# RWKV scores, chain and outputs of a two-layer hybrid mixer as products per head

## The chip, the cores and the metric

The kernel runs on one core of a Trainium2 chip. The metric is the device time of one execution in microseconds (us), as the median of several runs. The core has TensorE (PE; its weight loads are listed as PEld), VectorE (DVE), ScalarE (ACT), GpSimd (POOL) and the queue of SyncE (SP), from which most transfers are started. They run side by side and wait for each other by semaphores.

## What is computed

The reference is a network of two layers over 256 text and 1024 image tokens with 1024 channels. Each layer projects its normed input to four mixers (RWKV-7, S5, SSD and GLA), runs each in both directions over the tokens, and projects their outputs back. The change touches the RWKV mixer alone. It has 4 heads of 64 channels; for each direction and head a state S of 64 x 64 goes through the tokens, and the outputs of both directions are added:

```python
def step(S, inp):
    r_t, w_t, k_t, v_t, kk_t, a_t = inp
    sa = jnp.einsum('bhvk,bhk->bhv', S, -kk_t)
    S = S * w_t[:, :, None, :] + sa[..., None] * (kk_t * a_t)[:, :, None, :] + v_t[..., None] * k_t[:, :, None, :]
    y = jnp.einsum('bhvk,bhk->bhv', S, r_t) if need_out else None
    return S, y
...
y = ys[0] + ys[1]
```

A norm over each head, a bonus term and a gate follow. The kernel does the recurrence in chunks of 64 tokens: within a chunk as products with masked scores and the inverse of a triangular matrix, from chunk to chunk with S.

## The kernel before

A layer has three phases: the projections with the mixers other than RWKV and S5 (`project`), RWKV with S5 beside it (`rw`), and the projection out (`out_proj`). `rw` goes through 10 windows. A window is 128 tokens (two chunks, s = 0 and 1) of the forward direction and 128 of the backward one, whose tokens are reversed, so that both run as one. u = 0 to 3 counts direction (u // 2) and pair of heads (u % 2); a pair of heads h = 0, 1 fills the 128 partitions. Each window goes through five stages, and iteration i traces stage st of window i - st, in the order 3, 2, 4, 1, 0 (`ORDER`):

- stage 0, `rw_elem` (L1169): decays, keys and receptances by channel. It loads the window, makes two sets of decay products in the PSUM tag `ps`, whose results ScalarE's tanh reads (L1188), and writes `r_AR` (per chunk 64 columns of keys times decay and 64 of receptance times decay), `r_BK` and the decays `r_PM` of whole chunks;
- stage 1, `rw_pair` (L1232): the scores A of a chunk. GpSimd spreads AR into the zeroed tile `r_AD`, each head in its own columns and partitions (L1242); a product of 128 rows and 256 columns per chunk and pair of heads goes to the tag `pb` (L1246); VectorE masks it into `r_A` (L1248). Then the keys by token, `r_Bt`;
- stage 2, `rw_inv` (L1271), the inverses `r_TT`, with products of 32 x 32 in the tag `pi` and much VectorE work on `r_N`, `r_X` and `r_tp`, and `rw_vals` (L1330): the values into the lower half of `r_UV`, whose upper half GpSimd clears (L1346);
- stage 3, `rw_chain` (L1349): the recurrence over the two chunks. In `px`: a product with zeros that opens the bank (L1359), A times UV (L1362), AR times the state S (L1367). Two copies to `r_rs`, by VectorE and ScalarE (L1371, L1372). In `pu`: TT times rs (L1375), copied into the upper half of UV (L1376, L1377), and Bt times UV (L1382), added to the decayed state (L1389, L1390). Then the chunk's outputs by token, A times UV in the other half of px's rows (L1394), copied to `r_yw` (L1397);
- stage 4, `rw_out` (L1401): a product with the constant `IJ` (identity and reversed identity) turns yw to channels in a bank of `ps` and undoes the reversal of the backward direction (L1410); its result is copied or added into `r_yt` (L1419, L1421). `rw_final` (L1423) does norm, bonus and gate, when both directions have come to a block; it takes banks of `ps` too.

`PS` gives the PSUM banks by tag: px 2, pu 1, p5 1, pi 1, pb 2, ps 1. A new tile of a tag waits until a bank of it is free. All products are f32 and stand in the trace as two records each. Almost all are issued by the helper `mm` (L321), and elementwise work by `tt` (L333), `ts` (L336), `stt` (L339) and `act` (L330), so that lines say little and tiles are the better name. The order on each engine is not that of the text: the framework's planner (`schedule_with_timeline_sim`, L1810) lays it by priorities in the order of the text and its own estimate of times.

Of the kernel before, what the change touches and what calls it, by code (L numbers as in the profile page):

```python
# [11 lines left out]
F32 = mybir.dt.float32  # L12
# [20 lines left out]
# ---------------------------------------------------------------- column layout of w_in  # L33
# [30 lines left out]
# ---------------------------------------------------------------- per-layer parameter columns  # L64
# [24 lines left out]
for _d, _l in ((CON, [("ident", 128), ("ones", 128), ("bones", 128), ("eps", 1), ("gneps", 1), ("one", 1)]),  # L89
               (ACON, [("triF", 128), ("triB", 128), ("gmF", 64), ("gmB", 64), ("bm4", 4), ("c16", 16), ("reset64", 256)]),  # L90
               (RCON, [("IJ", 128), ("vinit", 256), ("rm", 128), ("m16", 32), ("reset64", 256)])):
    _o = 0
    for _n, _c in _l:
        _d[_n] = (_o, _c)
        _o += _c
# [6 lines left out]
def constants():  # L102
# [24 lines left out]
    ij = np.zeros((128, 128))  # L127
    ij[64:, :64] = np.eye(64)
    ij[:64, 64:] = np.eye(64)[::-1]
    put("IJ", ij)  # L130
# [93 lines left out]
# PSUM banks by tag: projections of the first layer and of the others, RWKV, out-projection  # L224
# [16 lines left out]
AA = "ppvv"  # L241
# engines of RWKV's elementwise work, by step: a ACT, p GpSimd, v DVE
EG = dict(bk="aa", ad="pppp", dg="aaaa", bb="pp", b0="p", b1="v", tk="pp", am="p", ar="vp", sp="p", bt="aa")
# [12 lines left out]
class K:  # L256
# [17 lines left out]
    def load_con(self, rwkv):  # L274
        """the constants and matrices of a phase"""
# [8 lines left out]
    def pools(self, es, nts=0, nq=0, nh=0, left=(), right=(), **psum):  # L284
        """the pools of a phase: by name, from either end of SBUF; PSUM banks by tag"""
# [23 lines left out]
    def ring(self, name, shape, n):  # L309
        """n tiles in turn, zeroed once: what is written later leaves the zeros alone"""  # L310
# [12 lines left out]
    # short names of engine operations  # L323
# [29 lines left out]
    def rsqrt(self, tag, in_, scale, eps):  # L353
        """1 / sqrt(in * scale + eps) of a few numbers per partition: a guess from the bits, Newton's steps"""
# [10 lines left out]
    def head_norm(self, tag, ps, sq, scale, eps):  # L365
        """ps: 1 / sqrt(mean of sq over its head + eps), by channel; its first columns hold the sums by token"""
# [8 lines left out]
    def y_out(self, Y, jobs, row, scale):  # L375
        """token-major Y (list of [128, 5, 256]) -> rows row.. of the stash, channels times scale[i]"""
# [12 lines left out]
    # ------------------------------------------------------------ GLA  # L389
    def gla(self, src, outs):  # L390
# [22 lines left out]
        for d in range(2):  # L413
# [16 lines left out]
            # chain factor of step s: exp(cs_mid of the next chunk + cs_last - cs_mid of this one)  # L430
# [21 lines left out]
        for s in range(20):  # L452
            ch = [s, 3 - s if s < 4 else 23 - s]
            jb = [x // 2 for x in ch]
            if s % 2 == 0:
                # keys by token, one half of the rows zero
# [11 lines left out]
            if s > 0 and (outs or s >= 4):  # L468
                # one direction is in the first half of its block of 128 tokens, the other in the second
# [15 lines left out]
            # state within each head; decayed, and spread over the columns of all heads  # L485
# [11 lines left out]
        # norm over each head, gate  # L497
# [16 lines left out]
    def gla_pair(self, j, qe, ke, pa, V, Y):  # L514
        """interactions within the two chunks of 128 tokens, both directions"""
# [22 lines left out]
    # ------------------------------------------------------------ SSD  # L538
    def ssd(self, src, outs):
        nc, c = self.nc, self.c  # L540
        jobs = list(range(0 if outs else 2, 10))
        # centred convolution in the padded axis, silu
# [12 lines left out]
        # strict triangles  # L555
# [4 lines left out]
        # dt and decays by token  # L560
# [16 lines left out]
        # the same in two parts  # L577
# [25 lines left out]
        # decays of the state by step, heads of a half of the partitions  # L603
# [7 lines left out]
        for s in range(10):  # L611
# [26 lines left out]
            # state within each head; spread over the columns of all heads  # L638
# [26 lines left out]
    def ssd_pair(self, j, B, C, cp, xt, stri, lap, dt, Y):  # L665
        """interactions within a chunk, both directions"""
# [6 lines left out]
        # decays of both directions: each leaves the other's triangle alone  # L673
# [37 lines left out]
    def s5_prep(self, l):  # L711
        """matrices of 8 tokens and phases of chunks for the scan, by quarters of 4 groups, out to DRAM"""
# [190 lines left out]
    def s5_jobs(self, outs):  # L903
# [7 lines left out]
        y = []  # L911
# [902 lines left out]
```

## Time and profile before

| | us |
|---|---|
| median of 3 runs | 2290.6 |
| lowest, highest | 2287.16, 2292.19 |
| span of the profiled execution | 2282.5 |
| PE busy in it | 1955.0 (86%) |
| DVE busy | 1565.4 (69%) |
| ACT busy | 933.8 (41%) |
| POOL busy | 830.7 (36%) |

The profile shows one execution from its first to its last instruction; the runs' time has also what lies around it. PE's time is the union of its records, whose ends are modelled. RWKV's phases are seen from the first load of decays to the last output: from 708 to 1142 us in the first layer and from 1768 to 2172 us in the second.

### The profile page before, as it was taken

The numbers are of one execution on the slowest core, as the hardware profiler recorded it, in microseconds if no ns is written. First come the engines' busy times: TensorE is split into PE (matmuls) and PEld (weight loads), VectorE is DVE, ScalarE is ACT, GpSimd is POOL, SyncE is SP. The second block draws the span as 40 slices with busy tenths as digits, with TensorE's granted clock in tenths as the row PEclk, the third lists the DMA queues.
The fourth block names the chain that finished last, engine by engine and source line by source line (L and its number), as shares of the span: only waits on it lengthen the run. The fifth ranks groups of instructions, "written<-read, shape, count | busy, mean of one in ns | idle before, by whom it ended". The sixth has DMA issues, their size and how long they took to land.

```text
span 2282.5 us, 44172 instructions
## 1 busy us (share of the span) xinstructions
PE 1955.0 (86%) x17176; PEld 1642.1 (72%) x17176; DVE 1565.4 (69%) x3513; ACT 933.8 (41%) x2016; POOL 830.7 (36%) x947
## 2 busy tenths in 40 slices
PE   7788898999975587878899999999996567888997
PEld 5577787778743466766799888887884456767797
DVE  3986867547495888897647724366665799987654
ACT  3445222223442554645423326122463456565420
POOL 1434753302246444553332203220136355454322
PEclk8689999999997688979999999999997678899898
DMA  8133544224454322422233423132412432220432
GB/s 281 44 116 122 179 152 136 65 91 140 149 164 136 112 83 80 121 64 68 94 116 94 137 90 133 55 99 86 146 50 73 145 97 85 80 75 25 139 112 93
DMA packets 208481, 246.79 MB, mean 108 GB/s; under 512 B 28816, under 2 KB 150672, under 8 KB 208272
## 3 DMA queue, kind: packets, MB, share of 16 engines
q1 hardware_dynamic: 175264, 215.52, 29.8%
q10 hardware_dynamic: 33008, 28.45, 3.8%
q8 instruction: 135, 2.21, 0.4%
q14 instruction: 74, 0.61, 0.1%
HBM read 169.29 MB, written 76.71 MB: 108 GB/s over the span
## 4 chain that ended last, share of the span: by engine, by line
PE 36%; DVE 17%; ACT 6%; issue 3%; DMA 3%; POOL 2%; SPq 0%; ACTq 0%; DVEq 0%; POOLq 0%
PE pj L321 22%; PE ps L321 3%; PE px L321 2%; PE pu L321 2%; DVE r_tp L333 2%; DVE r_X L333 2%; PE pb L321 2%; PE pc L321 1%; PE pi L321 1%; DVE r_N L1276 1%; DVE r_cs L1195 1%; PE p L321 1%; DVE z_x L333 1%; DVE r_BK L333 1%; ACT r_th L330 1%
## 5 line engine op out<-in xcount | busy, mean ns | idle before, releaser
L321 PE MATMUL pj<-hi,i_wh 128*128 128x512 f32 (+1 forms) x952 | 243.8, 377 | 18.6 <-DVE hi L1516 12.0
L321 PE MATMUL pj<-lo,i_wh 128*128 128x512 f32 (+1 forms) x952 | 240.2, 370 | 1.3 <-POOL lo L333 1.3
L321 PE MATMUL pj<-hi,i_wl 128*128 128x512 f32 (+1 forms) x952 | 239.1, 369 | 0.1
L321 PEld LDWEIGHTS pj<-hi,i_wh 128*128 128x128 f32 x952 | 169.1, 196 | 52.3 <-DVE hi L1516 12.4
L321 PEld LDWEIGHTS pj<-lo,i_wh 128*128 128x128 f32 x952 | 167.3, 193 | 32.5 <-issue 1.5
L321 PEld LDWEIGHTS pj<-hi,i_wl 128*128 128x128 f32 x952 | 167.0, 192 | 31.2 <-issue 2.6
L333 DVE TENSOR_TENSOR i_wl<-i_w,i_wh 128x512 fp32r<-128x512 f32 x108 | 82.6, 772 | 107.8 <-PE pj L321 59.9
L1539 ACT CAST i_wh<-i_w 128x512 fp32r<-128x512 f32 x108 | 66.4, 620 | 159.0 <-PE pj L321 113.4
L321 PE MATMUL pb<-r_AD,r_BK 128*128 128x256 f32 x320 | 99.9, 464 | 19.9 <-DVE r_tp L333 9.4
L321 PE MATMUL px<-r_UV,r_A 128*64 128x64 f32 x1216 | 103.9, 240 | 14.1 <-DVE r_UV L1376 10.5
L321 PEld LDWEIGHTS px<-r_UV,r_A 128*64 128x64 f32 x1216 | 88.1, 150 | 35.0 <-DVE r_UV L1376 14.6
L321 PEld LDWEIGHTS pb<-r_AD,r_BK 128*128 128x128 f32 x320 | 72.0, 237 | 37.6 <-issue 11.9
L333 DVE TENSOR_TENSOR r_X<-r_X,r_tp 128x30 f32<-128x30 f32 (+1 forms) x300 | 89.8, 299 | 6.7
L333 DVE TENSOR_TENSOR r_tp<-r_N,r_X 128x30 f32<-128x30 f32 (+1 forms) x300 | 87.6, 292 | 6.6
L321 PE MATMUL pu<-r_rs,r_TT 128*64 128x128 f32 x320 | 51.2, 311 | 35.0 <-ACT r_rs L1372 35.0
L330 ACT ACT_TABLE_LOAD x56 | 71.8, 1283 | 11.6 <-DMA z<-in_s5p 4.6
L330 ACT ACTIVATE i_o<-pj,omu 128x512 f32<-128x512 f32 (+1 forms) x46 | 28.5, 622 | 115.4 <-PE pj L321 113.8
L333 DVE TENSOR_TENSOR g_Y<-pc,g_Y 64x256 f32<-64x256 f32 x70 | 29.5, 421 | 65.0 <-ACT g_Y L536 35.3
L333 POOL TENSOR_TENSOR r_S<-r_S,r_PM 64x256 f32<-64x256 f32 x72 | 53.0, 737 | 56.6 <-DVE r_S L333 43.1
L321 PE MATMUL pj<-i_wh,hi 128*128 128x256 f32 x448 | 67.2, 288 | 6.4 <-ACT i_o L330 4.0
L336 POOL TENSOR_SCALAR r_AD<-r_AR 64x512 f32<-64x512 f32 (+1 forms) x80 | 56.7, 709 | 40.8 <-PE pb L321 31.9
L321 PEld LDWEIGHTS pu<-r_rs,r_TT 128*64 128x64 f32 x320 | 40.1, 155 | 41.4 <-ACT r_rs L1372 39.5
(458 smaller groups left out, 5172.6 us busy)
## 6 DMA issues: line engine op xcount, KB each, us to landing
i_w<-in_win SPq DMA_DIRECT2D x108, 256.0 KB, 3.0
i_o<-in_ada SPq DMA_DIRECT2D x96, 256.0 KB, 4.6
r_in<-rm SPq DMA_DIRECT2D x36, 512.0 KB, 4.2
rm<-i_o SPq DMA_DIRECT2D x48, 256.0 KB, 2.5
o_y<-yd SPq DMA_DIRECT2D x36, 256.0 KB, 3.2
z_st<-s5t SPq DMA_DIRECT2D x32, 256.0 KB, 2.7
o_w<-in_wout SPq DMA_DIRECT2D x32, 256.0 KB, 2.9
z_st<-s5t SPq DMA_DIRECT2D x24, 320.0 KB, 5.1
```

The costliest lines, as they stand in the source:

```text
L321: self.nc.tensor.matmul(out, lhsT, rhs, start=start, stop=stop, skip_group_check=True)
L330: self.nc.scalar.activation(out=out, in_=in_, func=f, **kw)
L333: (self.nc.vector if e == "v" else self.nc.gpsimd).tensor_tensor(out, a, b, op)
L336: (self.nc.vector if e == "v" else self.nc.gpsimd).tensor_scalar(out, a, s1, s2, op0, op1)
L1195: nc.vector.tensor_tensor_scan(cs[:, v], c("reset64"), t2[:, v], 0.0, OP.mult, OP.add)
L1276: nc.vector.transpose(Nt[:, :1024].rearrange("p (i j) -> p i j", j=32), AD.rearrange("p u t -> p t u").unsqueeze(2).to_broadcast([128, 32, ...
L1539: self.nc.scalar.copy(hi[:, v], w)
```

## The change

Comments and docstrings are left out of the new file; they are not shown. In `rw_pair`, r_AD and its copies go: each head's score product takes its own 64 partitions of BK and AR, 128 columns wide (64 in windows that give no outputs), and each head has its own bank. In `rw_chain` each product is taken per head with 64 output rows, which go to the lower or upper half of the bank's partitions by head; the opening product goes, rs is one tile of 128 partitions copied by VectorE alone, and the outputs leave the step. `rw_out` is called at the end of `rw_chain`: it makes the outputs by channel directly, S times the receptances and UV times A, and reverses the backward tokens when it writes them. IJ and yw go, UV has two buffers, S three.

```diff
@@ rw_pair
-        for d in range(2):
-            z = self.rzero("r_AD", [128, 2, 2, 2, 2, 64], 1)
+        hs = [slice(64 * h, 64 * h + 64) for h in range(2)]
+        for s in range(2):
+
+            ps = [self.P("pb").rearrange("p (u f) -> p u f", u=4) for _ in hs]
+            for u in range(4):
+                for h in range(2):
+                    self.mm(ps[h][:, u, :n], BK[hs[h], u, s].rearrange("p k t -> p (k t)"),
+                            AR[hs[h], u // 2, u % 2, s, :n // 64].rearrange("p k t -> p (k t)"))
             for h in range(2):
...
+                self.tt(A[:, s, :, h, :n], ps[h][:, :, :n], c("rm")[:, :n].unsqueeze(1).to_broadcast([128, 4, n]), OP.mult)
@@ rw_vals
-        UV = self.rzero("r_UV", [128, 2, 4, 128], 1)
+        UV = self.R("r_UV", [128, 2, 4, 128], 2)
@@ rw_chain
...
+            X = self.P("px")[:, :256].rearrange("p (u v) -> p u v", u=4)
+            for u, h in uh:
+                self.mm(X[hs[h], u], A[:, s, u, h, 0:64], UV[:, s, u, hs[h]], u == 0, S is None and u == 3)
             if S is not None:
...
+                for u, h in uh:
+                    self.mm(X[hs[h], u], AR[:, u // 2, u % 2, s, 0], S[:, u, hs[h]], False, u == 3)
+            rs = self.R("r_rs", [128, 4, 64], 2)
+            nc.vector.tensor_copy(rs, X)
+            ps = self.P("pu")[:, :256].rearrange("p (u v) -> p u v", u=4)
+            for u, h in uh:
+                self.mm(ps[hs[h], u], TT[hs[h], s * 4 + u], rs[hs[h], u])
+            nc.vector.tensor_copy(UV[0:64, s, :, hs[0]], ps[hs[0]])
+            nc.scalar.copy(UV[0:64, s, :, hs[1]], ps[hs[1]])
             Sn = None
...
+                X2 = self.P("pu")[:, :256].rearrange("p (u v) -> p u v", u=4)
+                for u, h in uh:
+                    self.mm(X2[hs[h], u], Bt[:, s, u, hs[h]], UV[:, s, u, hs[h]])
+
+                Sn = self.rzero("r_S", [128, 4, 128], 3)
...
             S = Sn
+        if need:
+            self.rw_out(W, at)
         return S
@@ rw_out
+        for s, S in enumerate(at):
+            for u in range(4):
+                o = ps[:, s, u % 2, u // 2]
+                if S is not None:
+                    for h in hs:
+                        self.mm(o[h], S[:, u, h], AR[:, u // 2, u % 2, s, 1], True, False)
+                for i, h in enumerate(hs):
+                    self.mm(o[h], UV[:, s, u, h], A[:, s, u, i, 64:128], S is None, True)
...
             if d:
-                o = o[:, :, ::-1]
+                o = o[:, :, ::-1, ::-1]
```

## Rows read from the trace of the kernel before

**Rows 1.** Busy us (instructions) of PE, PEld, DVE, ACT, POOL by stage, granted clock, DMA.
```profile
708.00:1142.00 434.00, 329.16 (x3891) 272.08 (x3892) 349.06 (x764) 224.15 (x532) 205.37 (x262) 0.83 0.29 90
1768.00:2172.00 404.00, 318.04 (x3812) 266.44 (x3811) 337.00 (x753) 219.13 (x522) 183.94 (x241) 0.84 0.30 92
```

**Rows 2.** Chain of waits from 708 to 1142 us, share of that stretch by line.
```profile
by line: issue 6.9%; PE px L321 6.1%; DVE r_tp L333 6.0%; DVE r_X L333 5.7%; PE pu L321 5.1%; PE pb L321 5.1%; PE ps L321 4.7%; PE pi L321 3.5%; PE p L321 3.5%; DVE r_N L1276 3.1%; DVE r_cs L1195 2.9%; ACT r_TT L1315 2.3%; DVE z_b L333 2.1%
```

**Rows 3.** Chain of waits from 1768 to 2172 us, share of that stretch by line.
```profile
by line: issue 8.6%; PE pu L321 6.8%; PE px L321 6.2%; DVE r_tp L333 5.5%; DVE r_X L333 5.3%; DVE z_x L333 3.4%; PE pb L321 3.3%; DVE r_BK L333 3.1%; DVE r_N L1276 2.9%; PE ps L321 2.6%; PE pi L321 2.5%; ACT r_th L330 2.5%; DVE r_cs L1195 2
```

**Rows 4.** Busy us by stage, as in the first group, for shorter stretches.
```profile
760.00:800.00 40.00, 26.46 (x276) 21.17 (x276) 38.74 (x76) 22.91 (x63) 19.90 (x28) 0.67 0.25 87
960.00:1000.00 40.00, 27.58 (x336) 22.84 (x335) 39.12 (x73) 17.66 (x44) 22.82 (x28) 0.79 0.15 47
1080.00:1120.00 40.00, 36.95 (x645) 31.14 (x644) 26.91 (x89) 18.15 (x40) 10.23 (x15) 0.99 0.13 42
1800.00:1880.00 80.00, 46.16 (x504) 37.61 (x508) 77.09 (x145) 40.14 (x103) 44.63 (x60) 0.71 0.32 95
1920.00:2000.00 80.00, 69.71 (x939) 60.45 (x943) 74.31 (x157) 39.85 (x102) 40.26 (x54) 0.84 0.28 84
```

**Rows 5.** Instructions in order of time: start, us, engine, out<-in, K*M, shape, records.
```profile
1079.01 1.15 PE L321 MATMUL px<-r_UV,r_A 128*64 128x64 f32 x16
...
1080.08 1.16 PE L321 MATMUL px<-r_S,r_AR 128*128 128x128 f32 x8
...
1081.17 1.15 PE L321 MATMUL px<-r_UV,r_A 128*64 128x64 f32 x16
...
1085.03 1.89 PE L321 MATMUL pb<-r_AD,r_BK 128*128 128x256 f32 x8
...
1086.85 0.68 PE L321 MATMUL px<-r_UV,r_A 128*64 128x64 f32 x8
...
1087.79 1.16 PE L321 MATMUL pu<-r_UV,r_Bt 128*128 128x128 f32 x8
...
1088.88 0.68 PE L321 MATMUL px<-r_UV,r_A 128*64 128x64 f32 x8
...
1098.38 1.09 PE L321 MATMUL ps<-con,qfy 128*64 128x128 f32 x16
...
1099.32 0.63 PE L321 MATMUL px<-r_UV,r_A 128*64 128x64 f32 x8
...
1107.56 1.09 PE L321 MATMUL pu<-r_rs,r_TT 128*64 128x128 f32 x8
...
1108.57 0.75 PE L321 MATMUL pi<-r_DN,r_Am 32*32 32x32 f32 x64
```

**Rows 6.** The same view: the two copies of px to rs in one step.
```profile
1105.91 0.41 DVE L1371 COPY r_rs<-px 64x256 f32<-64x256 f32 x1
...
1106.41 0.36 ACT L1372 COPY r_rs<-px 64x256 f32<-64x256 f32 x1 [2.78 <-DVE r_tp L333]
```

**Rows 7.** Chain of waits in order of time, one piece: start, us, what.
```profile
761.92 3.75 PE pb L321 x8
```

**Rows 8.** Groups by line: busy us, mean ns | idle before them, and its releasers.
```profile
L336 POOL TENSOR_SCALAR r_AD<-r_AR 64x512 f32<-64x512 f32 (+1 forms) x80 | 56.7, 709 | 40.8 <-PE pb L321 31.9 <-DVE r_AR L339 2.3 <-DVE r_AR L333 2.3
...
L1397 ACT COPY r_yw<-px 64x256 f32<-64x256 f32 x72 | 26.5, 369 | 50.4 <-PE px L321 49.9
...
L1346 POOL MEMSET r_UV<- 64x1024 f32 x20 | 18.9, 944 | 71.3 <-PE px L321 68.3 <-PE pu L321 3.0
```

**Rows 9.** Waits from 708 to 1142, then 1768 to 2172 us: total, times, longest.
```profile
ACT r_th L330 <- PE ps L321: 8.2, 6, 2.6
...
ACT r_th L330 <- PE ps L321: 20.0, 5, 16.2
```

**Rows 10.** Instructions in order of time: the copies into UV of two steps.
```profile
1083.92 0.41 DVE L1376 COPY r_UV<-pu 64x256 f32<-64x256 f32 x1 [2.23 <-PE pu L321]
...
1097.43 0.42 DVE L1376 COPY r_UV<-pu 64x256 f32<-64x256 f32 x1 [0.95 <-PE pu L321]
```

More of the change, by code (lines that the diff above doesn't have):

```diff
@@ L90 @@
                (ACON, [("triF", 128), ("triB", 128), ("gmF", 64), ("gmB", 64), ("bm4", 4), ("c16", 16), ("reset64", 256)]),
-               (RCON, [("IJ", 128), ("vinit", 256), ("rm", 128), ("m16", 32), ("reset64", 256)])):
+               (RCON, [("vinit", 256), ("rm", 128), ("m16", 32), ("reset64", 256)])):
     _o = 0
@@ L241 @@
 AA = "ppvv"
-EG = dict(bk="aa", ad="pppp", dg="aaaa", bb="pp", b0="p", b1="v", tk="pp", am="p", ar="vp", sp="p", bt="aa")
+EG = dict(bk="aa", dg="aaaa", bb="pp", b0="p", b1="v", tk="pp", am="p", ar="vp", sp="p", bt="aa")
 RN = (3, 2, 10)
@@ L1124, in rw @@
         self.rz = {}
-        for p, ns in (("re", "in th a cs eP BK AD Ad N X Am tp Rm Bb"), ("rx", "AR A"), ("rl", "ks yt fin f0 yw")):
+        for p, ns in (("re", "in th a cs eP BK Ad N X Am tp Rm Bb"), ("rx", "AR A"), ("rl", "ks yt fin f0")):
             self.where.update({"r_" + n: p for n in ns.split()})
@@ L1237, in rw_pair @@
         n = 128 if W["need"] else 64
-        for d in range(2):
-            z = self.rzero("r_AD", [128, 2, 2, 2, 2, 64], 1)
-            for h in range(2):
-                q = slice(64 * h, 64 * h + 64)
-                self.copy(EG["ad"][2 * d + h], z[q, :, :, h, :n // 64], AR[q, d, :, :, :n // 64])
-            for s in range(2):
-                ps = self.P("pb")
-                for hp in range(2):
-                    self.mm(ps[:, hp * 256:(hp + 1) * 256], BK[:, d * 2 + hp, s].rearrange("p k t -> p (k t)"),
-                            z[:, hp, s].rearrange("p h k t -> p (h k t)"))
-                self.tt(A[:, s, 2 * d:2 * d + 2].rearrange("p u h f -> p (u h) f"), ps.rearrange("p (a f) -> p a f", a=4),
-                        c("rm").unsqueeze(1).to_broadcast([128, 4, 128]), OP.mult)
+        hs = [slice(64 * h, 64 * h + 64) for h in range(2)]
[5 more added lines that the diff above has]
+                            AR[hs[h], u // 2, u % 2, s, :n // 64].rearrange("p k t -> p (k t)"))
+            for h in range(2):
+                self.tt(A[:, s, :, h, :n], ps[h][:, :, :n], c("rm")[:, :n].unsqueeze(1).to_broadcast([128, 4, n]), OP.mult)
         f = BK.rearrange("p u s k t -> p u s (k t)")
@@ L1352, in rw_chain @@
         w, need = W["w"], W["need"]
-        if need:
-            yw = W["yw"] = self.R("r_yw", [128, 2, 256], 1)
         hs = [slice(64 * h, 64 * h + 64) for h in range(2)]
+        uh = [(u, h) for u in range(4) for h in range(2)]
+        at = []
         for s in range(2):
-            last = w == 9 and s == 1
-            X = self.P("px").rearrange("p (u f) -> p u f", u=4)
-            self.mm(X.rearrange("p u f -> p (u f)"), self.zero[:, 0:128], self.zero, True, False)
-            for u in range(4):
-                for h in range(2):
-                    self.mm(X[0:64, u, hs[h]], A[:, s, u, h, 0:64], UV[:, s, u, hs[h]], False, False)
-            if S is not None:
-                for u in range(4):
-                    ar = AR[:, u // 2, u % 2, s]
-                    if need:
-                        self.mm(X[:, u], ar.rearrange("p k t -> p (k t)"), S[:, u], False, False)
-                    else:
-                        self.mm(X[0:64, u], ar[:, 0], S[:, u], False, u == 3)
-            rs = self.rzero("r_rs", [128, 4, 128], 2)
-            nc.vector.tensor_copy(rs[0:64, :, 0:64], X[0:64, :, 0:64])
-            nc.scalar.copy(rs[64:128, :, 64:128], X[0:64, :, 64:128])
-            ps = self.P("pu")[0:64].rearrange("p (u v) -> p u v", u=4)
-            for u in range(4):
-                self.mm(ps[:, u], TT[:, s * 4 + u], rs[:, u])
-            nc.vector.tensor_copy(UV[0:64, s, 0:2], ps[:, 0:2])
-            nc.scalar.copy(UV[0:64, s, 2:4], ps[:, 2:4])
-            Sn = None
-            if not last:
-                X2 = self.P("pu").rearrange("p (u f) -> p u f", u=4)
-                for u in range(4):
-                    self.mm(X2[:, u], Bt[:, s, u], UV[:, s, u])
-                Sn = self.rzero("r_S", [128, 4, 128], 2)
@@ new lines, in rw_chain @@
+            for u, h in uh:
+                self.mm(ps[hs[h], u], TT[hs[h], s * 4 + u], rs[hs[h], u])
+            nc.vector.tensor_copy(UV[0:64, s, :, hs[0]], ps[hs[0]])
+            nc.scalar.copy(UV[0:64, s, :, hs[1]], ps[hs[1]])
+            Sn = None
+            if not (w == 9 and s == 1):
+                X2 = self.P("pu")[:, :256].rearrange("p (u v) -> p u v", u=4)
+                for u, h in uh:
+                    self.mm(X2[hs[h], u], Bt[:, s, u, hs[h]], UV[:, s, u, hs[h]])
+                Sn = self.rzero("r_S", [128, 4, 128], 3)
@@ L1385, in rw_chain @@
                 for h in hs:
                     if S is None:
-                        nc.vector.tensor_copy(Sn[h, :, h], X2[h, :, h])
+                        nc.vector.tensor_copy(Sn[h, :, h], X2[h])
                     else:
                         self.tt(Sn[h, :, h], S[h, :, h], PM[h, s].unsqueeze(2).to_broadcast([64, 4, 64]), OP.mult, EG["sp"])
-                        self.tt(Sn[h, :, h], X2[h, :, h], Sn[h, :, h], OP.add)
-            if need:
-                for u in range(4):
-                    for h in range(2):
-                        self.mm(X[64:128, u, hs[h]], A[:, s, u, h, 64:128], UV[:, s, u, hs[h]], False, u == 3 and h == 1)
-                for d in range(2):
-                    o = yw[64:128, s] if d == 0 else yw[0:64, s]
-                    nc.scalar.copy(o, X[64:128, 2 * d:2 * d + 2].rearrange("p u f -> p (u f)"))
+                        self.tt(Sn[h, :, h], X2[h], Sn[h, :, h], OP.add)
@@ L1398, in rw_chain @@
             S = Sn
-        return S
-    def rw_out(self, W):
-        nc, c, bi = self.nc, self.c, W["bi"]
-        if not W["need"]:
-            return
-        b, first, yw = min(bi), self.rw_first(W, 0), W["yw"]
-        ps = self.P().rearrange("p (s a d t) -> p s a d t", s=2, a=2, d=2)
-        for s in range(2):
-            for hp in range(2):
-                self.mm(ps[:, s, hp].rearrange("p d t -> p (d t)"), yw[:, s, hp * 128:(hp + 1) * 128], c("IJ"))
+        if need:
+            self.rw_out(W, at)
@@ new lines, in rw_chain, with rw_out @@
+        return S
+    def rw_out(self, W, at):
+        nc, bi = self.nc, W["bi"]
+        A, AR, UV = [W[n] for n in ("A", "AR", "UV")]
+        b, first = min(bi), self.rw_first(W, 0)
+        hs = [slice(64 * h, 64 * h + 64) for h in range(2)]
+        ps = self.P().rearrange("p (s a d t) -> p s a d t", s=2, a=2, d=2)
+        for s, S in enumerate(at):
[6 more added lines that the diff above has]
+                    self.mm(o[h], UV[:, s, u, h], A[:, s, u, i, 64:128], S is None, True)
```

8 lines of the change are left out of this document (1 added, 7 removed).

## The prediction

> **What bounds the kernel now.** I read the busy time by stage first, then the chain of waits inside the two RWKV phases, then bursts of products in the order of time. Outside 708 to 1142 us and 1768 to 2172 us nothing is edited, so only these 838 us can move. In them VectorE is busy 686 us (82%), TensorE 647 us (77%) at a granted clock of 0.83 and 0.84, that is, some way between the levels 1.2 and 2.4 GHz; ScalarE has 53%, GpSimd 46% [rows 1]. No engine fills its time alone: windows wait on each other through a chain that runs over all of them. On the chain of waits the tiles that the edit touches hold px 6.1, pu 5.1 and pb 5.1% of the first phase's 434 us [rows 2] and 6.2, 6.8 and 3.3% of the second's 404 us [rows 3]: 70.7 + 65.9 = 137 us. So TensorE's products here are not hidden, and a shorter product has something to give. VectorE, though, is full in places: 97, 98, 96 and 93% in four stretches that hold 240 of the 838 us [rows 4]; there nothing is won that VectorE doesn't win.
>
> **Part 1: the chain's products.** An f32 product is two records on TensorE, so a count of 16 is eight products. I take costs from start to start, at the full clock. Now, a step costs: A times UV 1.07 us (1079.01 to 1080.08), S times AR 1.09 (to 1081.17), TT times rs 1.01 (1107.56 to 1108.57), Bt times UV 1.09 (1087.79 to 1088.88), and the output products, of the first one's shape, another 1.07 [rows 5]: 5.33 us. Two steps and the reversal product (eight records of 128 columns, by the 1.09 of S times AR) are 11.75 us a window; the zeroing product I count at nothing. After the edit each of the four products is 16 records of 64 columns, whose outputs alternate between the two halves of the columns. The trace before has that pattern once, with 128 columns: 16 records of the head norm in 0.94 us (1098.38 to 1099.32), 0.059 each, where TT times rs, without alternation, takes 1.01/8 = 0.126 for 128 columns [rows 5]. So two halves run side by side, and 64 columns cost 0.03: 0.47 for 16. Four products, two steps: 3.8 us. The 32 output products are 64 records: 1.9 us. Together 5.7 in place of 11.75.
>
> One of these four, TT times rs, also splits the rows, and both heads write one bank, pu. The nearest rows are the 32x32 products of the inverse: 64 records in 0.75 us, 12 ns each, four row groups into one bank pi [rows 5], where 64 columns on one place take 1.07/16 = 67 ns, 33 for 32 columns. So row groups there do overlap within a bank. The Trainium skill ("TensorEngine Tiling (Array Packing)", Gotcha 1) says that different row tiles cannot access one PSUM bank at the same time, which speaks against this product; by that rule TT times rs would stay at about 1.0 us, 40 steps lose 21 us of TensorE and, at the share of the path used below, the forecast would be some 9 us later. The trace here disagrees with the rule, so the sum goes by the row.
>
> **Part 2: the pair products.** Now 8 records of 256 columns take 1.82 us (1085.03 to 1086.85 [rows 5]), 3.64 a window. Afterwards 32 records of 128 columns, alternating between row halves, into two banks: 0.059 each if rows overlap as columns do, 1.9 us; 0.126 each if they don't, 4.0. Four row groups did overlap above, so I take 1.9.
>
> **Sum on TensorE.** 15.4 us a window become 7.6, some 7.8 less, 156 over 20 windows (two windows of the second layer, without outputs, give a little less). If nothing ran side by side it would be 16.9, 1.5 more a window. On the path I use the same share: 7.8/15.4 = 0.51 of 137 us, or **70 us less**; the bound without any overlap is 137 x 1.5/15.4 = 13 us more.
>
> **What comes back.** (a) In the four full stretches, 240/838 = 29% of the time, VectorE takes over at once: **20 us** of the 70 are not seen. (b) The clock. The less TensorE does, the lower its clock in this trace: busy 92% it had 0.99, 87% 0.84, 69% 0.79, 66% 0.67, 58% 0.71 [rows 4]. Its 647 us less 156/0.835 = 187 leave 460, or 57% of some 805 us: clock 0.71 by the nearest stretch. At half clock a burst doubles: eight pb records took 3.75 us at one place [rows 7], 1.89 at another [rows 5]. The TensorE lines named on the chain are 28.0% of 434 and 21.4% of 404 us [rows 2, 3], 208 us; less 70 leaves 138, times 0.835/0.71 - 1 = 0.18: **24 us more**. Its bounds are 0 (the clock stays) and 40 (0.65).
>
> **Part 3: other engines.** The copy of px into rs falls from VectorE and then ScalarE, one after the other (1105.91 to 1106.77 [rows 6]), to one copy of 256 columns on VectorE: 0.45 us less in each of 40 steps, 18 us; TensorE isn't always waiting for it, and I take half, **9 us**, between 0 and 18. The 80 GpSimd copies of AR into AD (56.7 us) and the 72 ScalarE copies into yw (26.5 us) go away [rows 8], and the clearing of UV, for which GpSimd stood idle 71.3 us behind px, no longer waits, as there are two buffers [rows 8]. These engines are about half busy, so I count nothing; what hides the loss or gain is the path over VectorE and TensorE, and the bound is a gain of some 10 us more. VectorE's own work doesn't change in size: the masks read as many columns, the copies as many, reversed writes included (taken at nothing; a bound is 18 windows times one 0.4 us copy, 7 us, if reversing doubled it). The third S buffer adds one clearing, at nothing. No DMA is moved.
>
> **Part 4: outputs earlier in the text.** They now stand in stage 3, ahead of the inverse, pair and elementwise stages, no longer in stage 4. In their bank, ps (one buffer), they are queued with the elementwise products and with the final norm: while it is open, the matrices of the next window's decays wait, and behind these ScalarE's two tanh. In the middle I take nothing for it.
>
> **Sum:** -70 + 20 + 24 - 9 = -35. The profiled execution's span of 2282.5 would be 2247; the median of the runs, 2290.6, lies 8 us above that span, and I let that stand: **2256 us**.
>
> **Rivals.** *Much faster (about 2210):* the freed TensorE, ScalarE and GpSimd let VectorE fill its gaps. The idle time of VectorE in both phases is 838 - 686 = 152 us; half of it is 76, so 2215. For it: PE holds nearly all of the tail (92% at 1080 to 1120 [rows 4]), and there the recurrence is short after the edit. Against it: the clock falls with use.
> *Hidden (2283 to 2293):* VectorE rules throughout and the chain's PE pieces were only filling; then 137 us of path mean little, and the 24 us of clock eat the rest. For it: 82% mean use. Against it: VectorE is at 67% in 1080 to 1120 [rows 4].
> *The edit doesn't do what it says:* row and column halves don't overlap for such short products; by the bound above +13 - 9 = 2295. Against it: the head norm's burst.
> *Slower, through the ps bank (about 2303):* the planner may open the outputs' bank with the first step's products and close it after the second step. Two steps' UV copies lie 13.5 us apart (1083.92 and 1097.43 [rows 10]), so the bank could be shut that long per window. ScalarE's tanh now waits 8.2 us in 6 times and 20.0 us in 5 times for products in ps [rows 9], 2.6 us each; once in each of 18 output windows on the path, that is +47: 2303. It decides against the edit from 35/18 = 1.9 us a window on. Against it: other windows' stages run in between, and elementwise work has a whole iteration of slack.
>
> **How the numbers follow.** Chances: forecast 0.52 (its own range 2236 to 2280), much faster 0.18, hidden 0.12, no overlap 0.06, ps bank 0.12. A measurement tells about 0.2%, here 4.6 us, from no change. The forecast and the fast case are faster by more, and of the hidden case about half (0.06): 0.76. Same: the other half and some of the no-overlap case, 0.09. Slower: 0.15. The range reaches from 2210 (in the middle of the fast case) to 2300, past the hidden case and the one without overlap and into the bank's; some 0.17 are left out.
>
> **What would show it.** Right: 16 px or pu records in about 0.7 us (0.47 and the pipeline's tail) at full clock; pb records of 128 columns, 16 in about 1 us; both phases shorter by 15 to 20 us each; VectorE's share in them near 86%; a clock near 0.71; no ScalarE record between px and pu. Wrong: 16 records still over 1 us (no overlap); phases of the same length with VectorE at 82% and long waits of ps for r_yt, or of r_th for ps (the bank); a clock under 0.65 with products as long as before.

## The result, and the profile after

The changed kernel takes 2323.3 us (median; 2319.5 to 2328.3) against 2291.1 us before on the same chip: 1.0156 times as long, interval 1.0128 to 1.0184. It is **slower by 36 us** by this ratio (32 by the two medians), where the forecast was 35 us faster. The profiled execution has a span of 2325.3 us, 43 above that of before. The page after, span and busy time of each engine:

```profile
span 2325.3 us, 47170 instructions
PE 1917.3 (82%) x18800; PEld 1608.2 (69%) x18800; DVE 1548.6 (67%) x3513; ACT 893.9 (38%) x1904; POOL 764.2 (33%) x859
```

Every engine does less than before, and the program ends later. Busy time by stage of the kernel after, columns as in [rows 1], over the two RWKV phases:

```profile
715.00:1159.00 444.00, 306.33 (x4711) 253.29 (x4712) 332.42 (x759) 199.12 (x466) 169.02 (x214) 0.73 0.27 83
1785.00:2213.00 428.00, 296.64 (x4604) 251.61 (x4605) 326.54 (x737) 201.03 (x472) 148.01 (x199) 0.71 0.28 87
```

These stretches last 872 us where [rows 1] has 838, but their ends are set by hand: the kernel before still copies outputs into r_yt until 1155 us, past the 1142 of [rows 1]. Counted in both kernels from the first scan r_cs to the last write of r_yt, the phases last 876 us before and 923 after, 47 more (10 in the first layer, 37 in the second), and the rest of the program is 4 us shorter. In the stretches above TensorE is busy 603 us (647 before), VectorE 659 (686), at a granted clock of 0.73 and 0.71 instead of 0.83 and 0.84. So there is less work and more waiting. The chain of waits of both phases, share of the stretch by line:

```profile
by line: issue 12.4%; PE ps L317 6.1%; DVE r_tp L329 6.0%; DVE r_X L329 5.6%; PE pb L317 4.3%; DVE r_N L1267 3.9%; PE p L317 3.1%; DVE r_cs L1188 2.9%; ACT r_TT L1306 2.5%; DVE z_x L329 2.5%; PE pi L317 2.5%; DVE z_b L329 2.4%; ACT r_th L32
by line: issue 10.1%; DVE r_tp L329 5.6%; DVE r_X L329 5.5%; PE ps L317 4.9%; PE p L317 4.7%; DMA o_w<-in_wout 3.4%; DVE r_cs L1188 3.2%; DVE r_N L1267 3.2%; PE pb L317 3.0%; PE pi L317 3.0%; DVE z_x L329 2.8%; PE pu L317 2.6%; DVE z_b L329
```

Against [rows 2, 3]: px is gone from the head of both lists and pu from the first, which is what the edit was to do. In its place stand ps (4.7 to 6.1% and 2.6 to 4.9%) and "issue" (6.9 to 12.4% and 8.6 to 10.1%), time for which the profile names no wait.

What stands in ps can be read in the order of time. The kernel after, one window's outputs and the decay products around them:

```profile
990.77 0.65 ACT L1404 COPY r_yt<-ps 128x256 f32<-128x256 f32 x2
991.47 1.16 PE L317 MATMUL ps<-r_in,rconm 128*128 128x128 f32 x8
994.94 1.05 PE L317 MATMUL ps<-r_in,rconm 128*128 128x128 f32 x8
997.48 0.34 PE L317 MATMUL ps<-r_AR,r_S 128*64 128x64 f32 x4
...
1047.74 0.65 ACT L1404 COPY r_yt<-ps 128x256 f32<-128x256 f32 x2
1048.44 1.16 PE L317 MATMUL ps<-r_in,rconm 128*128 128x128 f32 x8
1049.69 0.63 ACT L326 ACTIVATE r_th<-ps,r_sc 128x128 f32<-128x128 f32 x2
...
1054.65 1.27 DVE L1188 TENSOR_TENSOR_SCAN r_cs<-rcon,r_th 128x256 f32<-128x256 f32 x2 [0.52 <-ACT r_th L326]
```

The first output product opens the bank at 997.48. The copy that frees it ends at 1048.39, 51 us later, and 0.05 us after that the next window's decay products start; the same happened at 991.42 and 991.47. Behind them come ScalarE's tanh and then VectorE's scan r_cs, which here waits for the tanh. In the kernel before, where reversal products made the outputs in stage 4, the hold of the same (sixth) window reads:

```profile
1031.72 0.61 PE L321 MATMUL ps<-rcon,r_yw 128*128 128x128 f32 x4
...
1040.84 0.61 PE L321 MATMUL ps<-rcon,r_yw 128*128 128x128 f32 x4
1041.49 0.65 ACT L1419 COPY r_yt<-ps 128x256 f32<-128x256 f32 x2
1048.24 0.94 PE L321 MATMUL ps<-r_in,rconm 128*128 128x128 f32 x6
```

There the bank is shut for 10 us and then free for 6. Worked out so for all 18 windows with outputs, from the first output product to the end of the copy that frees the bank: before 184 us in all, 10.2 a window; after 404 us, 22.4 a window. Where decay products come next, they start within 0.15 us of the bank's release in 7 of 11 cases after, in 0 of 9 before.

### The profile page after: what moved, and what is told of

Its sections match the earlier page's. It is cut to its first block, busy times and chain, and to the rows that moved or that the text cites. A ratio compares the mean times of both kernels' runs of the same rounds, so it can differ in the third digit from the quotient of the medians.

```text
span 2325.3 us, 47170 instructions
## 1 busy us (share of the span) xinstructions
PE 1917.3 (82%) x18800; PEld 1608.2 (69%) x18800; DVE 1548.6 (67%) x3513; ACT 893.9 (38%) x1904; POOL 764.2 (33%) x859
## 4 chain that ended last, share of the span: by engine, by line
PE 42%; DVE 21%; ACT 7%; DMA 6%; issue 5%; POOL 2%; SPq 1%; DVEq 0%; ACTq 0%; POOLq 0%
PE pj L317 28%; PE ps L317 5%; PE pc L317 2%; DVE r_tp L329 2%; DVE r_X L329 2%; DMA o_w<-in_wout 2%; DMA i_o<-in_ada 2%; PE p L317 1%; PE pb L317 1%; DVE r_N L1267 1%; DVE r_cs L1188 1%; PE pi L317 1%; DVE z_x L329 1%; ACT r_TT L1306 1%; DMA o_y<-yd 1%
## 5 line engine op out<-in xcount | busy, mean ns | idle before, releaser
L317 PEld LDWEIGHTS pj<-hi,i_wh 128*128 128x128 f32 x952 | 167.7, 194 | 51.7 <-DVE hi L1501 12.4
L317 PE MATMUL pb<-r_AR,r_BK 64*128 64x128 f32 (+1 forms) x640 | 82.8, 372 | 34.4 <-DVE r_BK L329 16.2
L317 PEld LDWEIGHTS pb<-r_AR,r_BK 64*128 64x128 f32 x640 | 70.4, 263 | 43.4 <-POOL r_BK L329 19.2
L329 DVE TENSOR_TENSOR r_X<-r_X,r_tp 128x30 f32<-128x30 f32 (+1 forms) x300 | 77.7, 259 | 7.8
L329 DVE TENSOR_TENSOR r_tp<-r_N,r_X 128x30 f32<-128x30 f32 (+1 forms) x300 | 78.0, 260 | 7.3
L317 PE MATMUL ps<-r_A,r_UV 128*64 128x64 f32 x576 | 58.9, 266 | 27.8 <-DVE r_UV L1361 26.5
L326 ACT ACTIVATE r_BK<-r_BK,r_PM 128x128 f32<-128x128 f32 x160 | 55.7, 396 | 48.3 <-PE pb L317 47.1
L317 PEld LDWEIGHTS ps<-r_A,r_UV 128*64 128x64 f32 x576 | 50.4, 177 | 34.2 <-DVE r_UV L1361 28.9
L317 PE MATMUL ps<-r_in,rconm 128*128 128x128 f32 x320 | 57.5, 336 | 18.9 <-ACT r_a L326 13.0
L1306 ACT COPY r_TT<-r_DT 32x256 f32<-32x256 f32 x80 | 52.3, 653 | 51.5 <-DVE r_DT L329 50.6
```

The lines of the kernel that those rows point to most:

```text
L317: self.nc.tensor.matmul(out, lhsT, rhs, start=start, stop=stop, skip_group_check=True)
L326: self.nc.scalar.activation(out=out, in_=in_, func=f, **kw)
L329: (self.nc.vector if e == "v" else self.nc.gpsimd).tensor_tensor(out, a, b, op)
L1306: nc.scalar.copy(TT[q, :, 32 * b:32 * b + 32], DT[q].rearrange("p c u -> p u c"))
```

## Experiments

Each run is given as a ratio to the kernel before on the same chip. Differences between two runs are differences of these ratios times 2291 us. An interval is some 4 to 10 us to either side, so a difference between two runs of less than about 10 us tells little. Two theories stood against each other: the **bank** (the rival with a price on record: ps is shut too long), and that the scores per head, the lower clock or the mere order of the planner cost the time.

**A second bank for ps, taken from px.** The kernel's tags take eight banks in all, and the run keeps to eight, so one is given up. The two runs part the loss of px's bank from the gain of ps's.

```diff
-PS = dict(px=2, pu=1, p5=1, pi=1, pb=2, ps=1)
+PS = dict(px=1, pu=1, p5=1, pi=1, pb=2, ps=1)   # px_one
+PS = dict(px=1, pu=1, p5=1, pi=1, pb=2, ps=2)   # ps_two
```

> The changed kernel with px on one bank and nothing else: the control for the run with two ps banks. Theory bank: px is free again as soon as rs is copied, so one bank costs little, 2315 to 2340. If it comes out under 2300 the second ps bank is not what counts in the other run, and the order that the planner makes is.

> The changed kernel with one PSUM bank less for px (1) and one more for ps (2), so that the outputs' bank and the next window's decay products need not share one. Theory bank (the outputs open the only ps bank early and shut out the elementwise products): the 43 us by which the changed span is longer come back and some of the forecast gain with them, 2250 to 2285 us. Theory clock (TensorE does less, its clock falls from 0.83 to about 0.73 in the phases, and products on the path are slower): no better than 2310. Theory order (the planner's order of VectorE and SyncE is worse for another reason): anywhere from 2300 to 2330.

Measured: px one 1.0246 (1.0216 to 1.0276), ps two 1.0006 (0.9984 to 1.0028). On the same code the second ps bank is worth 55 us, and 34 against the changed kernel, which has the px bank. Both times lie on or just past the upper end of what the bank theory gave (2285.3 for up to 2285, 2343.5 for up to 2340). The second bank does what it should; the kernel with two banks in ps, in the order of time:

```profile
982.77 0.65 ACT L1404 COPY r_yt<-ps 128x256 f32<-128x256 f32 x2 [1.90 <-PE ps L317]
983.75 0.48 PE L317 MATMUL ps<-r_AR,r_S 128*64 128x64 f32 x4
984.16 2.08 PE L317 MATMUL ps<-r_in,rconm 128*128 128x128 f32 x8
```

Here the next outputs open one bank at 983.75 and decay products go on at 984.16 in the other.

**The same bank elsewhere.** If any eighth bank would do, ps is not the cause.

```diff
+PS = dict(px=1, pu=1, p5=1, pi=1, pb=3, ps=1)         # pb_three
+PS = dict(px=1, pu=1, p5=1, pi=1, pb=2, ps=1, po=1)   # po_own
-        ps = self.P().rearrange("p (s a d t) -> p s a d t", s=2, a=2, d=2)
+        ps = self.P("po").rearrange("p (s a d t) -> p s a d t", s=2, a=2, d=2)   # po_own
```

> The changed kernel with one px and three pb banks; compare with one px alone (2344). Theory pair banks: the third bank lets the next chunk start before the masks, 2305 to 2330. If the pb banks don't matter: 2338 to 2350.

> The changed kernel with one px bank and a bank of its own for the outputs; the decay products and the final norm keep the one ps bank. The outputs are traced in the chain as changed. Theory bank: what hurts is that the outputs share a bank with the decay products, so this is as good as two shared banks or better, 2255 to 2290. If the queue of TensorE is what hurts (output products ahead of others in the order), it stays at 2310 to 2345.

Measured: pb three 1.0162 (1.0126 to 1.0198), outputs in a bank of their own 1.0051 (1.0030 to 1.0071). Against px one, the eighth bank is worth 21 us in px (that is the changed kernel itself), 19 in pb, 45 as the outputs' own and 55 in ps. It is worth most where it separates the outputs from the decay products. The expectations were not all met: pb three (2326.1) falls into the range that the theory of the pb banks gave, so a third pb bank does bring something, and the outputs' own bank (2295.6) falls between the ranges of both theories.

**Outputs last in the iteration.** The bank stays single, but `rw_out` is called at the end of the iteration, after the next windows' stages, so that its products stand behind theirs in the planner's priorities.

```diff
-        if need:
-            self.rw_out(W, at)
+        W.update(at=at)
...
+            if 0 <= i - 3 < 10 and Ws[i - 3]["need"]:
+                self.rw_out(Ws[i - 3], Ws[i - 3]["at"])
```

> The changed kernel with the outputs' products traced at the end of the same iteration, after the elementwise stage, and not inside the chain; the same instructions, the same buffers. Theory bank: the decay products take the bank first and the outputs hold it more briefly, 2255 to 2290, with a hold per window near the 10 us of before and not the 22 us of after. Theory clock: as the changed kernel, 2315 to 2330. Theory order: uncertain, 2280 to 2330.

Measured: 1.0032 (1.0011 to 1.0054), 28 us less than the changed kernel; 2294.6 is above the bank's range and inside that of the order. The bank is now shut for 267 us, 14.9 a window, not near 10. Both means at once:

> Two ps banks and the outputs traced last in their iteration, both. Theory bank: they mend the same thing, so the sum is little better than two ps banks alone: 2275 to 2288. If they mended different things the gains would add up: 2245 to 2265.

Measured: **0.9875** (0.9841 to 0.9909), 2258.9 us: faster than both kernels, 64 us below the changed one. This is not what the bank theory gave (2275 to 2288). The gains add up: 34 and 28 make 62, and with two ps banks in place the late outputs still bring 30. By the expectation's own words the two means mend different things. What the late place mends, if not the shut bank, was not found. With the late outputs too, the eighth bank was tried in pb:

```diff
+PS = dict(px=1, pu=1, p5=1, pi=1, pb=3, ps=1)   # with the outputs last
```

> Outputs last with one px and three pb banks, one ps bank; compare with two ps banks and outputs last (2259) and with outputs last on the banks of the changed kernel (2295). If with late outputs the scores' banks are the next limit: 2255 to 2275. If the ps bank still is: 2280 to 2300.

Measured: 1.0116 (1.0071 to 1.0161), 2311.2 us, slower than both ranges. With eight banks and the same order of the text, ps two against pb three is 55 us; with the outputs early it is 36.

**Was it a limit before?** Before, with px one and ps two:

> The kernel before with one px and two ps banks. In it the outputs still hold a bank for 10 us a window, and px is held to the end of the step's outputs. If the ps bank was a limit before the change too, and not a cost that the change brought: 2250 to 2280. If the change brought it: 2285 to 2330, since one px bank makes the next step wait for the copies to yw.

Measured: 1.0061 (1.0043 to 1.0078). The bank moved from px to ps there costs 14 us. So ps was not worth a px bank in the kernel before. The control with one px bank alone was not run there, so this does not price the ps bank by itself. The nearest pair of runs is the kernel before with the scores per head (below): there the second ps bank brings 12 us over its control, where it brings 55 in the changed kernel.

**The planner's own noise.** An edit that changes nothing but the order in which four pairs of heads are written out in `rw_out`:

```diff
-            for u in range(4):
+            for u in (3, 2, 1, 0):
```

> The changed kernel with the output products of a chunk written in the opposite order of u; same instructions, same waits. It shows how far an edit without meaning moves the time through the planner's order. Theory bank and theory clock: 2315 to 2332. If the order alone is what rules: anything between 2285 and 2345.

> Two ps banks and outputs last (2259), with the output products of a chunk written in the opposite order of u: an edit without meaning. If the 2259 stands on the banks and the place of the outputs: 2252 to 2268. If it was a lucky order: 2270 to 2290.

Measured: 1.0155 (1.0130 to 1.0181) in the changed kernel, 0.9857 (0.9815 to 0.9898) in the fastest one. Neither moves by more than 5 us. This edit only permutes products within one group, though; the next section has a bank taken away that gains 33 us, so an effect of the planner's order of that size is not excluded for any single run above. What speaks against it is that the second ps bank is better than the same bank elsewhere with the outputs early and late.

**The scores per head.** Alone on the kernel before (its `rw_pair` as changed, all else as before), and undone in the changed kernel:

```diff
-        for d in range(2):
-            z = self.rzero("r_AD", [128, 2, 2, 2, 2, 64], 1)
+            ps = [self.P("pb").rearrange("p (u f) -> p u f", u=4) for _ in hs]   # pair_only; pair_old the reverse
```

> The kernel before with only the scores per head (64-row products, no AD copies); chain and outputs as before. Theory bank: this part holds no ps bank, so it should give its share of the forecast, 5 to 20 us: 2270 to 2286. Theory clock: about 35 us less TensorE work lower the clock a little, 2285 to 2300.

> The changed kernel with the scores as before (AD copies, products of 128 rows and 256 columns, one bank per direction and chunk); chain and outputs as changed. Theory pair banks (a chunk's scores now fill both pb banks, so the next chunk's products and the key transposes wait for two masks in VectorE's queue): the 42 us that the scores alone cost come back in good part, 2275 to 2300. Theory clock: TensorE does more, clock up, 2295 to 2315. If the cost of the scores alone was an accident of that order: 2315 to 2335.

> The same with one px and two ps banks. Theory bank together with theory pair banks: both costs gone, so the forecast's gain shows, 2235 to 2265. If one of the two is wrong: 2270 to 2290, no better than with two ps banks alone.

> Two ps banks, outputs last, and the scores as before (AD copies, products of 256 columns). If the scores per head are worth nothing or less even here: 2250 to 2262. If they are worth their share of the forecast once the outputs don't block: 2265 to 2285.

Measured: alone 1.0191 (1.0157 to 1.0225); undone in the changed kernel 1.0024 (1.0002 to 1.0046); undone with ps two 0.9997 (0.9973 to 1.0021); undone in the fastest kernel 0.9975 (0.9958 to 0.9992). So the scores cost 44 us on the kernel before, 30 us in the changed one, nothing (2 us) with ps two, and bring 23 us in the fastest. Alone, 5 to 20 us of gain were expected. Undone in the changed kernel the time (2295.6) falls into the range of the pair banks, and with ps two (2286.0) into that of "one of the two is wrong".

This is also the strongest evidence against the shut bank as the whole cause. In the changed kernel with the old scores the outputs are as early and their bank is shut almost as long: 386 us, 21.4 a window. The sixth window's outputs there, in the order of time:

```profile
1002.31 0.34 PE L317 MATMUL ps<-r_AR,r_S 128*64 128x64 f32 x4 [0.24 <-ACT r_a L326]
...
1038.39 0.65 ACT L1406 COPY r_yt<-ps 128x256 f32<-128x256 f32 x2 [1.68 <-PE ps L317]
1039.09 1.16 PE L317 MATMUL ps<-r_in,rconm 128*128 128x128 f32 x8
```

The bank is shut for 37 us, and the decay products come 0.05 us after its release, as in the changed kernel. Yet this kernel is 30 us faster, and a second ps bank brings it only 6 us, within the noise. The other way round, px one has a shorter hold than the changed kernel (19.8 a window) and is 21 us slower. So a long hold alone does not cost the time; in these runs it costs where the scores are per head as well. Why the two need each other was not found.

My guess for the scores was that they need both banks of pb at once. In the kernel with the scores alone, VectorE's masks and the score products read:

```profile
990.32 1.16 PE L321 MATMUL pb<-r_AR,r_BK 64*128 64x128 f32 x16
996.73 1.29 DVE L333 TENSOR_TENSOR r_A<-pb,rcon 128x512 f32<-128x512 f32 x2
997.47 2.09 PE L321 MATMUL pb<-r_AR,r_BK 64*128 64x128 f32 x16 [3.14 <-DVE r_A L333]
1008.56 0.69 DVE L333 TENSOR_TENSOR r_A<-pb,rcon 128x512 f32<-128x512 f32 x1
1009.28 0.68 DVE L333 TENSOR_TENSOR r_A<-pb,rcon 128x512 f32<-128x512 f32 x1
```

The second chunk's products wait for the first chunk's masks, and its own masks come 9 us after the products, behind S5's work and the inverses' in VectorE's queue. Three more runs put that guess to the test:

> The kernel before with the scores per head and one px bank, seven banks in use: the control for the two runs of it with an eighth bank for ps or pb (2288, 2286). If the eighth bank is what mends them: 2325 to 2350. If it is the order, which any change of banks shuffles: 2280 to 2300.

> The kernel before with the scores per head, one px and two ps banks; compare with the scores per head alone (2331). If the scores per head are slow because elementwise work comes late behind the ps bank: 2270 to 2300. If because of the two pb banks or the order: 2320 to 2350.

> The kernel before with the scores per head, one px and three pb banks. If they are slow because a chunk's scores fill both pb banks: 2285 to 2315. If not: 2325 to 2350.

Measured: px one 1.0045 (1.0021 to 1.0068), ps two 0.9992 (0.9972 to 1.0012), pb three 0.9984 (0.9958 to 1.0011). The last two fall into the ranges that their theories gave, but the control takes that away: *taking a bank away* from px gives 33 us, and the eighth bank then gives 12 in ps and 14 in pb alike. What costs 44 us in the first of these kernels is thus no want of a bank; that it is an unlucky order of the planner fits, but was only argued. The null edits above don't show such a large swing. This stays open.

**The clock.** The fastest kernel, with eight bf16 products of zeros, 256 columns wide, ahead of each step of the chain, into the half of px that nothing reads. They compute nothing.

```diff
-            X = self.P("px")[:, :256].rearrange("p (u v) -> p u v", u=4)
+            X = self.P("px")
+            for _ in range(8):
+                self.mm(X[:, 256:512], self.zero[:, 0:128], self.zero[:, 0:256])
+            X = X[:, :256].rearrange("p (u v) -> p u v", u=4)
```

> The run with two ps banks and outputs last (2259), with eight bf16 products of zeros of 256 columns more in each chain step, into the unused half of px's bank; their results are overwritten by nothing and read by nobody. They do no work but keep TensorE moving. Theory clock: the clock in the phases rises from 0.75 towards 0.85, and the products on the path that run at half clock shorten: 2235 to 2252. If the clock is no price here: 2259 to 2285, the products of zeros being in the way.

Measured: 1.0013 (0.9989 to 1.0036), 2289.7 us, 32 us slower than without and past both ranges. Busy time by stage of both, without the zero products first:

```profile
712.00:1136.00 424.00, 312.17 (x4839) 257.24 (x4840) 343.36 (x801) 200.92 (x472) 176.57 (x225) 0.76 0.30 94
1746.00:2156.00 410.00, 298.72 (x4614) 249.43 (x4615) 330.92 (x768) 204.74 (x475) 154.87 (x205) 0.74 0.30 94
```

```profile
712.00:1151.00 439.00, 322.47 (x4980) 262.15 (x4978) 346.81 (x799) 199.84 (x470) 172.91 (x225) 0.78 0.28 89
1760.00:2185.00 425.00, 318.20 (x4793) 263.34 (x4792) 336.50 (x779) 203.87 (x475) 168.37 (x212) 0.74 0.29 92
```

The clock barely rose (0.76 to 0.78, and 0.74 stayed), so the run doesn't tell what the clock costs. One burst lasts 1.05 us, 42 us over 40 steps, which would account for the loss if most of it lay on the path; that was not measured. The price of the clock stays open.

## Why the prediction was wrong, step by step

**The step that failed** is in Part 4: "In the middle I take nothing for it", of the outputs' earlier place and their bank. In its place the runs showed losses: a second ps bank brings 34 us back although px gives one up for it, a bank of the outputs' own 24, the outputs last in the text 28, and two ps banks with late outputs 64. The mechanism was on record as the rival "Slower, through the ps bank", with its place (first step's products open, second step's close) and its condition, 1.9 us a window. It is right that the bank is shut for long (22.4 us a window) and that the next window's decay products start right after its release. Its chance of 0.12 rested on "a whole iteration of slack"; where those products start within 0.15 us of the release, in 7 of 11 cases, no slack is seen. Its price, 2.6 us a window from the waits of r_th in [rows 9], made 47 us; the second bank, net of px, brings 34, or 1.9 a window.

**A second term failed with it**: the scores' share of the 70 us in the sum. Their TensorE work shrank as forecast, but alone they cost 44 us on the kernel before, and undoing them brings 30 us in the changed one. The two losses overlap: with two ps banks and the old scores 36 us come back, not 34 + 30. Why the scores cost time, and why the shut bank costs it only beside them, stays open.

**The sign that I named for it** was wrong, too. I looked for long waits of ps for r_yt, or of r_th for ps. The waits after, 708 to 1190 us and then 1776 to 2256 us (total, times, longest):

```profile
ACT r_th L326 <- PE ps L317: 9.9, 8, 2.2
...
PE ps L317 <- ACT r_yt L1404: 0.4, 1, 0.4
...
ACT r_th L326 <- PE ps L317: 26.4, 5, 21.7
```

Against [rows 9] that is 8 us more in all, and hardly a wait for r_yt. (These stretches are longer than those of [rows 9]; the kernel before has no further wait of r_th for ps up to 1190 and 2210 us.) My reading is that the planner, which plans for the shut bank, lays other work ahead on TensorE, so that the decay products come up just when the bank is freed (0.05 us in the rows above). The loss is then in the order, where a list of waits doesn't show it. This is argued, not shown: the time from the first write of a bank to its last read shows that the bank is shut, but, as the kernel with the old scores tells, not what that costs.

**Part 1, the chain's products: right.** The kernel after, in the order of time:

```profile
816.07 0.68 PE L317 MATMUL pu<-r_rs,r_TT 64*64 64x64 f32 x16
...
818.34 0.69 PE L317 MATMUL pu<-r_UV,r_Bt 128*64 128x64 f32 x16
...
886.99 1.16 PE L317 MATMUL pb<-r_AR,r_BK 64*128 64x128 f32 x16
...
1027.82 0.42 DVE L1357 COPY r_rs<-px 128x256 f32<-128x256 f32 x1
1028.30 1.12 PE L317 MATMUL pu<-r_rs,r_TT 64*64 64x64 f32 x16 [4.70 <-DVE r_rs L1357]
```

16 records last 0.68 and 0.69 us, as forecast ("about 0.7"). TT times rs, whose two row halves write one bank (each its own partitions), is as short as Bt times UV, which has no row halves; so the rule weighed there (the Trainium skill, "TensorEngine Tiling (Array Packing)", Gotcha 1) is not borne out by this product. In the last line the same burst takes 1.12 us; the granted clock there is 0.5, the lower level.

**Part 2, the pair products: right.** 16 records of 128 columns in alternating row halves last 1.16 us, 0.07 each, where 0.126 was the price without overlap; "about 1" was forecast. So the row halves overlap here. That is the price on TensorE only; the gain in time did not follow, as said above.

**Sum on TensorE: two thirds.** Busy time times granted clock is 647 x 0.835 = 540 us before and 306 x 0.73 + 297 x 0.71 = 434 after: 106 us less at full clock, not 156. The bursts have their forecast length; I take the rest for their tails, which count at each of the now more numerous, shorter groups, but this was not measured by itself.

**What comes back: (b) right in level by luck, (a) wrong.** The clock is 0.73 and 0.71 (0.71 forecast). But the forecast took it from a stretch in which TensorE was busy 58%, and TensorE is busy 603/872 = 69% now, where [rows 4] has 0.79 at 69%; and those rows do not fall evenly (0.67 at 66%, 0.71 at 58%). Its cost of 24 us was not separated. VectorE's share is 659/872 = 76%, not 86%: VectorE didn't take over as the limit.

**Part 3: right where it can be seen.** The rs copy is one record of 0.42 us by VectorE, with no ScalarE record between px and pu. The reversed writes cost nothing that can be seen: the copies into r_yt last 0.65 us for two, before and after.

**The sum.** The kernel with two ps banks and late outputs takes 2258.9 us, 3 us from the forecast of 2256. That is as likely luck as proof: this kernel has one px bank less and its outputs where Part 4 did not put them, its two gains add up against the bank theory, and the part of the scores alone ran from 44 us lost to 23 us won with what stood around it. Of the other rivals, the one without overlap falls with the bursts, "hidden" took VectorE as the limit that rules, which at 76% it was not, and "much faster" wanted VectorE's 152 us of idle time halved, and it grew to 872 - 659 = 213.

## What to carry to other kernels

When work is moved ahead, ask of each PSUM bank not only who writes it but how long it stays shut, from the first product to the last read, and who stands next in line; a group of products whose parts become ready one after the other shuts its bank for the whole of that time. The hold is a suspicion and not yet a price: here the same long hold cost 34 us beside one form of the scores and nothing to be seen beside the other. So try one bank more at the suspect against the same bank elsewhere, and try it with the other parts of the change undone as well. When two cures are meant to mend one thing, write down beforehand what their sum should be, and take the answer when they add up. A change whose products became as short as forecast and whose time is worse may be worth a second look at where its parts stand: here the same products, with one bank moved and one call later, are 1.2% faster than before.

## What the runs showed of the hardware that I had not expected

VectorE's small operations in the inverses, which the edit doesn't touch, became shorter. Groups by line (busy us, mean ns | idle before them), the kernel before and then the kernel after:

```profile
L333 DVE TENSOR_TENSOR r_X<-r_X,r_tp 128x30 f32<-128x30 f32 (+1 forms) x300 | 89.8, 299 | 6.7
L333 DVE TENSOR_TENSOR r_tp<-r_N,r_X 128x30 f32<-128x30 f32 (+1 forms) x300 | 87.6, 292 | 6.6
```

```profile
L329 DVE TENSOR_TENSOR r_X<-r_X,r_tp 128x30 f32<-128x30 f32 (+1 forms) x300 | 77.7, 259 | 7.8
L329 DVE TENSOR_TENSOR r_tp<-r_N,r_X 128x30 f32<-128x30 f32 (+1 forms) x300 | 78.0, 260 | 7.3
```

The 600 operations of the same shapes take 177 us before and 156 after; over the experiments they range from 146 us (px one) to 182 (the fastest kernel with the old scores). GpSimd's total load does not explain it: GpSimd is busy 831 us before and 764 after, but 823 us go with 155 us in the kernel with the scores undone. What counts is whether a GpSimd instruction runs at that moment. Two places of the kernel before:

```profile
842.05 1.53 POOL L333 TENSOR_TENSOR z_t<-z_b,z_st 128x640 f32<-128x640 f32 x1 [2.70 <-issue]
842.13 1.52 DVE L333 TENSOR_TENSOR r_tp<-r_N,r_X 128x30 f32<-128x30 f32 x1
843.68 0.22 DVE L333 TENSOR_TENSOR r_X<-r_X,r_tp 128x30 f32<-128x30 f32 x1
...
892.68 1.04 POOL L333 TENSOR_TENSOR r_f<-r_yt 128x512 f32<-128x512 f32 x1 [3.87 <-DVE r_yt L339]
892.75 1.03 DVE L333 TENSOR_TENSOR r_X<-r_X,r_tp 128x44 f32<-128x44 f32 x1
893.82 0.20 DVE L333 TENSOR_TENSOR r_tp<-r_N,r_X 128x40 f32<-128x40 f32 x1
```

The small VectorE operation that starts just after a GpSimd instruction ends with it; its neighbours of the same size take 0.2 us. Of the 600 operations, 195 overlap a GpSimd instruction before and 144 after; these last 513 and 475 ns on average, the others 191 and 192 and never more than 224. Every one that lasts over 0.4 us, 101 before and 57 after, ends within 0.15 us of the end of a GpSimd instruction. So an operation of 0.2 us on VectorE can take as long as the GpSimd instruction beside it. The difference of some 22 us comes from the overlaps, by 195 x 322 ns = 63 us against 144 x 283 = 41, and it is most of the 27 us that VectorE's busy time fell in the phases. It did not decide the case: px one has the shortest of these operations and is the slowest kernel.
